# Decoder trunk on one core: a block's first weight chunk multiplied k tile by k tile, and the squares of the norm issued behind the split of x

## The chip, the cores and the metric

The kernel runs on one core of a Trainium2 chip, in one launch. The metric is the device time of one execution in microseconds (us). Input x has 256 tokens of width 1024 and stays on the chip from the first block to the last; what streams in from memory is 350 MB of weights in float32. The engines are TensorE (PE, matmuls; PEld is its weight load), VectorE (DVE), ScalarE (ACT), GpSimd (POOL) and SyncE (SP, which issues the DMAs).

## What is computed

Four layers, each of three residual steps. Mixer i mod 3 is a gated DeltaNet (layers 0 and 3, "gdn" below), a stick-breaking attention (layer 1, "sb") and a sparse attention with an indexer (layer 2, "dsa").

```python
def rmsnorm(x, g):
    y = xf * lax.rsqrt(jnp.mean(xf * xf, axis=-1, keepdims=True) + NORM_EPS)
    return (y * g).astype(x.dtype)

def swiglu(h, w_gu, w_down):
    gate, up = jnp.split(h @ w_gu, 2, axis=-1)
    return (jax.nn.silu(gate) * up) @ w_down

for i in range(DEPTH):                                   # 4
    x = x + 0.5 * swiglu(rmsnorm(x, ffn1_norm[i]), ffn1_w_gu[i], ffn1_w_down[i])
    x = x + mixer[i % 3](rmsnorm(x, mix_norm[i]))
    x = x + 0.5 * swiglu(rmsnorm(x, ffn2_norm[i]), ffn2_w_gu[i], ffn2_w_down[i])
return rmsnorm(x, final_norm)
```

D_MODEL is 1024 (8 k tiles of 128, `KT`) and D_FF is 2816.

## The kernel before

There are twelve blocks in a row, three for each layer: ffn1, mixer, ffn2. They are named here ffn1_0, gdn, ffn2_0, ffn1_1, sb, ffn2_1, ffn1_2, dsa, ffn2_2, ffn1_3, gdn (the second) and ffn2_3.

**Arithmetic.** A float32 product is made of three one-pass matmuls: both operands are split into a high part and a low part, and high x high, low x high and high x low are added in PSUM. A weight chunk is 128 x 2048 numbers; its DMA fills a raw tile `r`, and each quarter is split by ACT (L175, `h<-r`) and DVE (L176, `l<-r,h`). x is kept as eight tiles of 128 x 256. At the start of a block each of them is scaled by the gain and split by `norm_tile`: ACT writes the high part (L227) and DVE the low part (L228). One tile of products (`tile_wide`, 128 output rows by 256 tokens) is then 8 k tiles x 3 matmuls = 24 matmuls into a PSUM bank "G", of which there are four. ACT and DVE evict it (L340, L341).

**From block to block.** The last chunk of a block runs in `rows` with `last` set: after each x tile's last matmul, DVE adds the result to x (L313), and the order of the k tiles, `korder`, is the order in which the next block takes them. So the eight L313 of one block, the eight L227 and L228 of the next, and the first 24 matmuls of the next run one behind the other, a tile at a time.

**The norm.** The scale of each token (`rstd`) isn't needed for the first matmuls; it is applied to their results later. `rstd` squares x on ACT (four L249, each over two x tiles), adds the four pairs on POOL (L250 to L253, three of 128 x 512 and one of 128 x 256), sums over partitions by matmuls with a matrix of ones (rows `bankA<-ones,sq`), takes mean and inverse root on DVE (L259, then L213 to L217; in dsa a power on POOL, L262), spreads the result over the partitions by two transposes (L56, `bankA<-ident,rs_y`), and copies it to `rb` on ACT (L268). In an ffn block the evicted tiles wait for `rb`: L353 to L355 and the split of the result (L204, L205 into `ah`, `al`) stand behind it, and the first down-projection matmuls (`bankA<-ah,h`) behind those.

**What sets the order.** `rstd` is a generator that sits in a list of side work. `pump`, called after every second k tile, advances it when its due time has come on a clock `now` that counts matmul columns; `lat_sum` (5.2) is the delay between the squares and the sum, and `lat` (4.6, in an ffn block 6.6) that between the sum and the spread. The framework's scheduler then gives each engine one fixed program order; an engine takes its instructions in that order, and one that waits holds all behind it. Without a rule of its own a square (L249) is placed as soon as its two x tiles are up to date.

The first block (ffn1_0) loads x from memory and has its own start (`first_chunk`); gdn starts with eight groups of three small matmuls (16 output rows, `bah`, `bal`), sb with a product in which x is the moving operand and has 512 columns, and dsa with `project(1)` and `project(0)`, two calls of `tiles2` (two M tiles one after the other in one bank).

Of the kernel before, what the change touches and what calls it, by code (L numbers as in the profile page):

```python
# [16 lines left out]
AF = mybir.ActivationFunctionType  # L17
# [3 lines left out]
P = 128  # L21
T = 256
D = 1024
KT = D // P
# [41 lines left out]
class Trunk:  # L66
# [157 lines left out]
    def norm_tile(self, xg, n, j):  # L224
        g = self.gains[:, n, j:j + 1]
        xh, xl = xg[j]
        self.nc.scalar.activation(xh, self.x[:, j], AF.Copy, scale=g)  # L227
        self.nc.vector.scalar_tensor_tensor(xl, self.x[:, j], g, xh.bitcast(F32), op0=ALU.mult, op1=ALU.subtract)  # L228

    def norm_in(self, n):  # L230
# [13 lines left out]
    def rstd(self, st, lat=4.6, power=False):  # L244

        nc = self.nc
        sq = self.b8("sq")
        for j in range(4):
            nc.scalar.activation(sq[:, 2 * j:2 * j + 2], self.x[:, 2 * j:2 * j + 2], AF.Square)  # L249
        nc.gpsimd.tensor_add(sq[:, 0:2], sq[:, 0:2], sq[:, 2:4])  # L250
        nc.gpsimd.tensor_add(sq[:, 0:2], sq[:, 0:2], sq[:, 4:6])
        nc.gpsimd.tensor_add(sq[:, 0:2], sq[:, 0:2], sq[:, 6:8])
        nc.gpsimd.tensor_add(sq[:, 0], sq[:, 0], sq[:, 1])  # L253
        yield self.lat_sum
        b = self.bank()
        for t in range(2):
            b.mm(b.t[:, t * P:(t + 1) * P], sq[:, 0, t * P:(t + 1) * P], self.ones)
        a = self.small("ms", [P, 2])
        nc.vector.tensor_scalar(a, b.v4()[:, :2, 0], 1.0 / D, EPS, op0=ALU.mult, op1=ALU.add)  # L259
        if power:  # L260
            y = self.small("rs_y2", [P, 2])
            nc.gpsimd.tensor_tensor(y, a, self.half, op=ALU.pow)  # L262
        else:
            y = self.rsqrt(a, 2)
        yield lat
        s = self.spread([y[:, t:t + 1] for t in range(2)])
        rb = self.small("rb", [P, T])
        nc.scalar.activation(rb, s.t[:, :T], AF.Copy)  # L268
        st["rstd"], st["rb"] = y, rb
# [1 line left out]

    pool_lo = ()
    lag, width, burst = 1.0, 6, 5
    lat_sum, lat_power = 5.2, 2.4
    dsa_width = 4
    g_key, g_val, g_qry, g_del, g_new, g_inv, g_out, g_mul = 9.0, 6.0, 6.0, 8.0, 2.8, 1.0, 7.5, 1.0
    s_qk, s_sp, s_att = 2.5, 5.5, 1.3
# [2 lines left out]
                 (2, 1), (3, 2), (2, 2), (2, 3), (3, 3))  # L280
    korder = (0, 2, 4, 6, 1, 3, 5, 7)

    def tiles2(self, pieces, xg, order=None):

        b = self.bank("G")
        for m in range(2):
            for q, j in enumerate(order or self.korder):
                b.mm3(b.t[:, m * T:(m + 1) * T], self.sub(pieces, m * D + j * P, P), xg[j], q == KT - 1)
                if q % 2:
                    self.pump()  # L290
        return b

    def tile_wide(self, pieces, m, order=None):

        b = self.bank("G")
        for q, j in enumerate(order or self.korder):
            wh, wl = self.sub(pieces, m * D + j * P, P)
            xh, xl = self.x2[:, j, :T], self.x2[:, j, T:]
            b.mm(b.t[:, :T], wh, xh, False)
            b.mm(b.t[:, T:], wl, xh, False)  # L300
            b.mm(b.t[:, T:], wh, xl, q == KT - 1)
            if q % 2:
                self.pump()
        return b
# [15 lines left out]
    def ffn(self, w, n, first=False, done=None):  # L320
        nc = self.nc
        if first:
            c0, xg = self.first_chunk(w[0, 0], n)
        else:
            c0, xg = None, self.norm_in(n)
# [4 lines left out]
        def gu(s):  # L330
            for f in range(2):
                order = range(KT) if first and s + f == 0 else None
                c = c0 if c0 and s + f == 0 else self.chunk(w[s, f], parts=4 if first and s == 0 else 1)
                if first and s == 0 and f:
                    for t, src in self.consts:
                        nc.sync.dma_start(t, src)
                e = self.w5("e")
                for m in range(2):
                    b = self.tile_wide(c, m, order=order)
                    nc.scalar.activation(e[:, m * T:(m + 1) * T], b.t[:, :T], AF.Copy)  # L340
                    nc.vector.tensor_add(e[:, m * T:(m + 1) * T], e[:, m * T:(m + 1) * T], b.t[:, T:])  # L341
                late.append(e)
                if first and s + f == 0:
                    self.add(self.rstd(st, 6.6))
                if s > 0:
                    self.wait(lambda: "rb" in st)
                if "rb" in st:
                    while late:
                        acts.append(act(late.pop(0)))
# [419 lines left out]
    def dsa(self, n):  # L769
        nc, a = self.nc, self.a  # L770
# [8 lines left out]
        xg = self.norm_in(n)  # L779
# [8 lines left out]
        sq = self.b8("sq")  # L788
# [171 lines left out]
            self.split(oh[:, h], ol[:, h], bo.t[:, :T])  # L960
            heads[h] = (oh[:, h], ol[:, h])

        def project(c):
            return self.tiles2(self.chunk(a["dsa_in"][c]), xg)

        def project_q(hf):
            pieces = self.chunk(a["dsa_uq"][hf], 1536, 384)
# [7 lines left out]
                self.add(queries(2 * hf + e, b))  # L975


        b1, b0 = project(1), project(0)
        self.wait(lambda: "rb" in st)
        latents(1, b1)  # L980
        self.add(factor("fk", 2, (3,), 64, ones64, fk), 1.5)
# [6 lines left out]
        pieces = self.chunk(a["dsa_qidx"], 1536, 384)  # L988
        for pr in range(4):
            b = self.bank("G")  # L990
# [8 lines left out]
        pieces = self.chunk(a["dsa_uk"], 1536, 384)  # L999
        self.wait(lambda: {"fkv", "kidx"} <= fl)  # L1000
        for hp in range(4):
            b = self.bank("G")
# [12 lines left out]
        pieces = self.chunk(a["dsa_uv"])  # L1015
        self.width = self.dsa_width
        for t in range(2):
            ts = slice(t * P, (t + 1) * P)
            for hf in range(2):
                b = self.bank("G")  # L1020
# [197 lines left out]
```

## Time and profile before

| | us |
|---|---|
| runs | 2082.24, 2075.12, 2054.35 |
| median of the runs | 2075.12 |
| the profiled execution | 2066.59 |
| its span in the profile | 2064.6 |
| PE busy in it | 2009.8 (97%) |
| DVE, ACT, POOL busy | 1603.2 (78%), 1305.8 (63%), 163.8 (8%) |

The rows below are of the profiled execution. In a timeline row the first number is the start in us from the span's start, the second the duration; "x2" groups neighbours; matmuls overlap, so a row's duration (0.28 us) is longer than the distance to the next (0.11 to 0.12 us), and the distance of two starts is what a matmul costs. In brackets stands how long the engine was idle before the row and what released it. "a <- b: 4.9, 9, 0.7" in the view of the waits means that a waited for b for 4.9 us in all, 9 times, at most 0.7 us. The chain of waits follows the work that ended last backwards through whatever released it.

### The profile page before, as it was taken

The page shows a single profiled execution, that of the slowest core. Times are in us where ns is not written, and L with a number is a line of the kernel's source. Part 1 is how long each engine was busy: PE and PEld are TensorE (multiplying, and loading weights), DVE is VectorE, ACT ScalarE, POOL GpSimd, SP SyncE. Part 2 cuts the span into 40 slices and gives each one's busy share as a digit, 9 for nine tenths or more (in the row PEclk, how much of TensorE's full clock was granted, in tenths as well). Part 3 has the DMA queues.
Part 4 walks back from the last instruction along what each step waited for, and adds up shares of the span by engine and source line. Part 5 has one row for each costly group of instructions (what it writes and reads, how often), then busy time and mean ns, then how long its engine had stood idle before and what let it go on. Part 6 is the DMA issues. An engine that isn't in the chain of part 4 may idle for free.

```text
span 2064.6 us, 43653 instructions
## 1 busy us (share of the span) xinstructions
PE 2009.8 (97%) x17578; PEld 1978.6 (96%) x17578; DVE 1603.2 (78%) x3413; ACT 1305.8 (63%) x2804; POOL 163.8 (8%) x150
## 2 busy tenths in 40 slices
PE   8999899999999999999999998999999998999998
PEld 8999889999999989999999997999999998999998
DVE  8778898877877776866787779877787789988665
ACT  6656776666666666655666665666666667766554
POOL 1001411100100010100010023100010014201000
PEclk9999999999999999999999999999999999999999
DMA  7554323555555543555555542455555543235552
GB/s 273 191 199 170 107 104 124 184 195 193 180 209 186 202 168 139 196 184 184 184 190 199 187 161 88 165 187 201 189 195 190 198 170 103 103 123 184 184 184 82
DMA packets 52619, 353.93 MB, mean 171 GB/s; under 512 B 6976, under 2 KB 7872, under 8 KB 10688
## 3 DMA queue, kind: packets, MB, share of 16 engines
q1 hardware_dynamic: 52128, 350.49, 47.9%
q8 instruction: 137, 2.24, 0.4%
q10 hardware_dynamic: 288, 0.66, 0.1%
q14 instruction: 66, 0.54, 0.1%
HBM read 350.07 MB, written 1.05 MB: 170 GB/s over the span
## 4 chain that ended last, share of the span: by engine, by line
PE 83%; DVE 11%; ACT 3%; issue 2%; POOL 1%; DMA 0%; SPq 0%; ACTq 0%; DVEq 0%; POOLq 0%
PE bankG L43 56%; PE bankA L43 26%; DVE l L176 4%; ACT x L227 1%; DVE kT L477 1%; PE bankA L56 1%; ACT h L175 1%; DVE x L228 1%; DVE qT L477 0%; DVE x L313 0%; DVE rs_y L217 0%; DVE vT L477 0%; DVE pc L466 0%; DVE rs_t L215 0%; ACT sq L249 0%
## 5 line engine op out<-in xcount | busy, mean ns | idle before, releaser
L43 PE MATMUL bankG<-x,h 128*128 128x256 f32 x7008 | 1257.3, 280 | 9.1 <-ACT x L227 6.1
L176 DVE TENSOR_TENSOR l<-r,h 128x512 fp32r<-128x512 f32 x1328 | 936.2, 713 | 398.9 <-ACT h L175 396.8
L175 ACT ACTIVATE h<-r 128x512 fp32r<-128x512 f32 x1328 | 822.1, 626 | 575.7 <-PE bankG L43 329.1
L43 PEld LDWEIGHTS bankG<-x,h 128*128 128x128 f32 x7008 | 1077.6, 189 | 11.5 <-ACT x L227 6.4
L43 PE MATMUL bankG<-x,l 128*128 128x256 f32 x3504 | 978.4, 279 | 0.1
L43 PEld LDWEIGHTS bankG<-x,l 128*128 128x128 f32 x3504 | 659.9, 188 | 0.4 <-DVE l L176 0.3
L43 PE MATMUL bankA<-ah,h 128*128 128x256 f32 x1408 | 390.9, 278 | 0.0
L43 PE MATMUL bankA<-al,h 128*128 128x256 f32 x1408 | 390.9, 278 | 0.0
L43 PE MATMUL bankA<-ah,l 128*128 128x256 f32 x1408 | 390.8, 278 | 0.0
L43 PEld LDWEIGHTS bankA<-al,h 128*128 128x128 f32 x1408 | 266.0, 189 | 0.1
L43 PEld LDWEIGHTS bankA<-ah,h 128*128 128x128 f32 x1408 | 264.4, 188 | 0.1
L43 PEld LDWEIGHTS bankA<-ah,l 128*128 128x128 f32 x1408 | 264.4, 188 | 0.0
L341 DVE TENSOR_TENSOR e<-e,bankG 128x256 f32<-128x256 f32 x352 | 145.5, 414 | 0.9 <-ACT e L340 0.9
L340 ACT ACTIVATE e<-bankG 128x256 f32<-128x256 f32 x352 | 133.3, 379 | 7.9 <-PE bankG L43 6.3
L250 POOL TENSOR_TENSOR sq<-sq 128x512 f32<-128x512 f32 x12 | 15.5, 1290 | 1445.0 <-ACT sq L249 1445.0
L353 DVE TENSOR_TENSOR e<-e,rb 128x512 f32<-128x512 f32 x176 | 119.8, 685 | 0.0
L204 ACT ACTIVATE ah<-e 128x256 fp32r<-128x256 f32 x176 | 73.2, 417 | 22.1 <-DVE e L355 22.0
L354 ACT ACTIVATE e<-e 128x256 f32<-128x256 f32 x176 | 70.9, 404 | 14.3 <-DVE e L353 14.3
L355 DVE TENSOR_TENSOR e<-e 128x256 f32<-128x256 f32 x176 | 73.6, 419 | 0.5 <-ACT e L354 0.5
L205 DVE TENSOR_TENSOR al<-e,ah 128x256 fp32r<-128x256 f32 x176 | 73.6, 419 | 0.5 <-ACT ah L204 0.5
L43 PE MATMUL bankG<-oh,h 128*128 128x256 f32 x256 | 73.1, 286 | 0.1
L43 PE MATMUL bankG<-oh,l 128*128 128x256 f32 x256 | 71.3, 279 | 0.0
(292 smaller groups left out, 1683.0 us busy)
## 6 DMA issues: line engine op xcount, KB each, us to landing
r<-in_ffn SPq DMA_DIRECT2D x262, 1024.0 KB, 4.8
r<-in_gdn_in SPq DMA_DIRECT2D x32, 1024.0 KB, 4.8
r<-in_gdn_out SPq DMA_DIRECT2D x8, 1024.0 KB, 4.8
r<-in_sb_qk SPq DMA_DIRECT2D x8, 1024.0 KB, 4.8
r<-in_sb_v SPq DMA_DIRECT2D x4, 1024.0 KB, 5.0
r<-in_sb_out SPq DMA_DIRECT2D x4, 1024.0 KB, 4.8
r<-in_dsa_out SPq DMA_DIRECT2D x4, 1024.0 KB, 5.3
r<-in_dsa_in SPq DMA_DIRECT2D x3, 1024.0 KB, 4.8
```

What stands on the lines that cost most here:

```text
L43: self.nc.tensor.matmul(out, lhsT, rhs, start=self.fresh, stop=stop, skip_group_check=True)
L56: self.nc.tensor.transpose(out, x, self.k.ident)
L175: self.nc.scalar.activation(h[:, :pw], src, AF.Copy)
L176: (self.nc.gpsimd if pool else self.nc.vector).tensor_sub(l[:, :pw], src, h[:, :pw].bitcast(F32))
L204: self.nc.scalar.activation(dh, src, AF.Copy)
L205: self.nc.vector.tensor_sub(dl, src, dh.bitcast(F32))
L227: self.nc.scalar.activation(xh, self.x[:, j], AF.Copy, scale=g)
L340: nc.scalar.activation(e[:, m * T:(m + 1) * T], b.t[:, :T], AF.Copy)
L341: nc.vector.tensor_add(e[:, m * T:(m + 1) * T], e[:, m * T:(m + 1) * T], b.t[:, T:])
L353: nc.vector.tensor_mul(e2, e2, st["rb"][:, None, :].to_broadcast([P, 2, T]))
L354: nc.scalar.activation(e[:, :T], e[:, :T], AF.Silu)
L355: nc.vector.tensor_mul(e[:, T:], e[:, T:], e[:, :T])
```

## The change

Three things are edited. In the ffn blocks except ffn1_0, the first two output tiles are computed by `first_pair`: for each k tile the six matmuls of both M tiles, into two G banks, where before one M tile's 24 matmuls came first and then the other's. dsa's first product gets the same treatment inside one bank (`tiles2` with `first`). The four squares of `rstd` are issued under `issue_after(self.last_act)`, behind the L227 of the last x tile. And `lat_sum` goes from 5.2 to 6.5. Nothing is added or left out of the arithmetic; the number of instructions on each engine stays.

```diff
@@ norm_tile
-        self.nc.scalar.activation(xh, self.x[:, j], AF.Copy, scale=g)
+        self.last_act = self.nc.scalar.activation(xh, self.x[:, j], AF.Copy, scale=g).ins
@@ rstd
-        for j in range(4):
-            nc.scalar.activation(sq[:, 2 * j:2 * j + 2], self.x[:, 2 * j:2 * j + 2], AF.Square)
+        with self.tc.issue_after(self.last_act):
+            for j in range(4):
+                nc.scalar.activation(sq[:, 2 * j:2 * j + 2], self.x[:, 2 * j:2 * j + 2], AF.Square)
@@
-    lat_sum, lat_power = 5.2, 2.4
+    lat_sum, lat_power = 6.5, 2.4
@@ tiles2
+        if first:
+            for q, j in enumerate(self.korder):
+                w = [self.sub(pieces, m * D + j * P, P) for m in range(2)]
+                for i, o in ((0, 0), (1, 0), (0, 1)):
+                    for m in range(2):
+                        b.mm(b.t[:, m * T:(m + 1) * T], w[m][i], xg[j][o], q == KT - 1 and o == 1)
+                self.pump()
+            return b
@@
+    def first_pair(self, pieces):
+
+        bs = [self.bank("G") for _ in range(2)]
+        for q, j in enumerate(self.korder):
+            xh, xl = self.x2[:, j, :T], self.x2[:, j, T:]
+            w = [self.sub(pieces, m * D + j * P, P) for m in range(2)]
+            for m, b in enumerate(bs):
+                b.mm(b.t[:, :T], w[m][0], xh, False)
+                b.mm(b.t[:, T:], w[m][1], xh, False)
+            for m, b in enumerate(bs):
+                b.mm(b.t[:, T:], w[m][0], xl, q == KT - 1)
+            self.pump()
+        return bs
@@ ffn
+                pair = self.first_pair(c) if s + f == 0 and not first else None
                 for m in range(2):
-                    b = self.tile_wide(c, m, order=order)
+                    b = pair[m] if pair else self.tile_wide(c, m, order=order)
@@ dsa
-        b1, b0 = project(1), project(0)
+        b1 = project(1, True)
+        b0 = project(0)
```

**PE, start of ffn2_0.** The first row is the last matmul of the mixer's output projection; `x_5538` is the split x of ffn2_0. Before:

```order
L43 MATMUL bankG<-ol,h 128x256
L43 MATMUL bankG<-x_5538,h 128x256
L43 MATMUL bankG<-x_5538,l 128x256
L43 MATMUL bankG<-x_5538,h 128x256 x2
L43 MATMUL bankG<-x_5538,l 128x256
L43 MATMUL bankG<-x_5538,h 128x256 x2
```

Of the change, the same place:

```order
L43 MATMUL bankG<-ol,h 128x256
L43 MATMUL bankG<-x_5538,h 128x256
L43 MATMUL bankG<-x_5538,l 128x256
L43 MATMUL bankG<-x_5538,h 128x256
L43 MATMUL bankG<-x_5538,l 128x256
L43 MATMUL bankG<-x_5538,h 128x256 x3
L43 MATMUL bankG<-x_5538,l 128x256
L43 MATMUL bankG<-x_5538,h 128x256
L43 MATMUL bankG<-x_5538,l 128x256
L43 MATMUL bankG<-x_5538,h 128x256 x3
```

Each x tile now feeds six matmuls in a row in place of three. Further down, the matmuls with the ones (`bankA<-ones,sq`) stand behind 72 matmuls of the block in place of 60, and the spread behind 140 in place of 128; the first down-projection matmul stays behind 196.

**ACT, start of ffn2_0.** `x_5538` is L227's output, `sq` the squares, `h` a weight piece, `e` an eviction. Before:

```order
L227 ACTIVATE x_5538<-x,gains 128x256 x4
L175 ACTIVATE h<-r 128x512
L227 ACTIVATE x_5538<-x,gains 128x256
L249 ACTIVATE sq<-x 128x512
L227 ACTIVATE x_5538<-x,gains 128x256 x2
L249 ACTIVATE sq<-x 128x512
L227 ACTIVATE x_5538<-x,gains 128x256
L249 ACTIVATE sq<-x 128x512 x2
L175 ACTIVATE h<-r 128x512
L340 ACTIVATE e<-bankG 128x256
```

Of the change (the squares are now L250, the eviction L364):

```order
L227 ACTIVATE x_5538<-x,gains 128x256 x4
L175 ACTIVATE h<-r 128x512
L227 ACTIVATE x_5538<-x,gains 128x256
L175 ACTIVATE h<-r 128x512
L227 ACTIVATE x_5538<-x,gains 128x256 x2
L175 ACTIVATE h<-r 128x512
L227 ACTIVATE x_5538<-x,gains 128x256
L250 ACTIVATE sq<-x 128x512 x4
L175 ACTIVATE h<-r 128x512 x3
L364 ACTIVATE e<-bankG 128x256 x2
```

The places of the first two squares, ahead of the last three x tiles, are taken by two weight pieces; all four squares follow the eighth x tile.

**ACT, start of the first gdn.** `x_2669` is its split x. Before:

```order
L227 ACTIVATE x_2669<-x,gains 128x256
L249 ACTIVATE sq<-x 128x512
L227 ACTIVATE x_2669<-x,gains 128x256 x2
L249 ACTIVATE sq<-x 128x512
L227 ACTIVATE x_2669<-x,gains 128x256
L249 ACTIVATE sq<-x 128x512 x2
L175 ACTIVATE h<-r 128x512
L162 ACT_TABLE_LOAD
```

Of the change:

```order
L227 ACTIVATE x_2669<-x,gains 128x256
L175 ACTIVATE h<-r 128x512
L227 ACTIVATE x_2669<-x,gains 128x256 x2
L162 ACT_TABLE_LOAD
L227 ACTIVATE x_2669<-x,gains 128x256
L250 ACTIVATE sq<-x 128x512 x4
L175 ACTIVATE h<-r 128x512 x7
```

Here a load of ACT's function table has moved ahead of the eighth x tile. In sb and dsa it stands right behind the eighth x tile and ahead of all four squares; before, two squares stood ahead of it. In gdn the sum keeps its place behind 72 matmuls and the spread behind 96; in sb the sum moves from 36 to 42 and the spread from 54 to 58, in dsa from 60 to 72 and from 86 to 98.

## Rows read from the trace of the kernel before

**Rows 1.** The page's line of the clock granted to PE, in 40 slices of the span (9 is 90% of full speed or more).

```profile
PEclk9999999999999999999999999999999999999999
```

**Rows 2.** The view of the waits, whole span: what PE waited for at the spread, and its weight loads at block starts (us in total, times, longest us).

```profile
PE bankA L56 <- DVE rs_y L217: 11.5, 10, 2.2
...
PEld bankG L43 <- DVE x L228: 4.9, 9, 0.7
```

**Rows 3.** The timeline of PE in ffn2_0: its first matmul, the matmul at the eighth x tile and the next one, the sum of squares, and the first down-projection matmul.

```profile
373.99 0.28 PE L43 MATMUL bankG<-x,h 128*128 128x256 f32 x1
...
376.58 0.28 PE L43 MATMUL bankG<-x,l 128*128 128x256 f32 x1
377.06 0.51 PE L43 MATMUL bankG<-x,h 128*128 128x256 f32 x2 [0.20 <-DVE x L228]
...
381.39 0.60 PE L43 MATMUL bankA<-ones,sq 128*128 128x128 f32 x4
...
397.05 0.28 PE L43 MATMUL bankA<-ah,h 128*128 128x256 f32 x1
```

**Rows 4.** The timeline of ACT at the start of ffn2_0.

```profile
373.42 0.61 ACT L249 ACTIVATE sq<-x 128x512 f32<-128x512 f32 x1
373.94 0.89 ACT L227 ACTIVATE x<-x,gains 128x256 fp32r<-128x256 f32 x2
374.74 0.61 ACT L249 ACTIVATE sq<-x 128x512 f32<-128x512 f32 x1
375.26 0.49 ACT L227 ACTIVATE x<-x,gains 128x256 fp32r<-128x256 f32 x1
375.66 1.14 ACT L249 ACTIVATE sq<-x 128x512 f32<-128x512 f32 x2
```

**Rows 5.** The timelines of DVE and of POOL there, one after the other; the last DVE row is the split of a result that the down projection takes first.

```profile
375.79 1.22 DVE L228 SCALAR_TENSOR_TENSOR x<-x,gains,x 128x256 fp32r<-128x256 f32 x1 [0.29 <-ACT x L227]
376.93 1.78 DVE L176 TENSOR_TENSOR l<-r,h 128x512 fp32r<-128x512 f32 x1
...
393.73 0.42 DVE L205 TENSOR_TENSOR al<-e,ah 128x256 fp32r<-128x256 f32 x1
...
375.43 1.29 POOL L250 TENSOR_TENSOR sq<-sq 128x512 f32<-128x512 f32 x1 [32.92 <-ACT sq L249]
376.80 1.36 POOL L251 TENSOR_TENSOR sq<-sq 128x512 f32<-128x512 f32 x1
378.24 1.63 POOL L252 TENSOR_TENSOR sq<-sq 128x512 f32<-128x512 f32 x1
379.94 1.07 POOL L253 TENSOR_TENSOR sq<-sq 128x256 f32<-128x256 f32 x1
```

**Rows 6.** The chain of waits (start us, us, what): long pieces of it with nothing but PE, ahead of ffn2_0, in ffn2_0 and in ffn2_1.

```profile
362.84 9.56 PE bankG L43 x81
...
402.65 10.88 PE bankG L43 x96
...
874.32 11.31 PE bankG L43 x96
```

**Rows 7.** The view by stretches, ffn2_1 and then ffn1_2 from after their start to before their end (stretch, its length, and then for each engine busy us and instructions, PEclk, share of DMA, GB/s).

```profile
845.00:1031.00 186.00, 185.62 (x1577) 185.42 (x1576) 137.04 (x266) 112.20 (x231) 5.36 (x4) 1.00 0.53 187
1033.00:1212.00 179.00, 178.79 (x1576) 178.59 (x1575) 136.68 (x265) 111.72 (x230) 5.34 (x4) 1.00 0.55 193
```

**Rows 8.** Timelines at the start of the first gdn: ACT's second square and its table load, POOL's last add, and PE at the eighth x tile, at the sum and at the spread.

```profile
191.22 0.61 ACT L249 ACTIVATE sq<-x 128x512 f32<-128x512 f32 x1
...
193.82 1.28 ACT L162 ACT_TABLE_LOAD   x1
...
196.41 1.07 POOL L253 TENSOR_TENSOR sq<-sq 128x256 f32<-128x256 f32 x1
...
193.55 0.29 PE L43 MATMUL bankA<-x,bah 128*16 128x256 f32 x1 [0.17 <-DVE x L228]
...
199.21 0.61 PE L43 MATMUL bankA<-ones,sq 128*128 128x128 f32 x4
...
203.01 0.43 PE L56 MATMUL bankA<-ident,rs_y 128*128 128x128 f32 x2 [0.60 <-DVE rs_y L217]
```

**Rows 9.** Timelines at the start of sb (the first four) and of dsa (the others): POOL's last add, the sum and the spread on PE, and ACT's squares behind its table load.

```profile
742.70 1.07 POOL L253 TENSOR_TENSOR sq<-sq 128x256 f32<-128x256 f32 x1
...
743.93 0.61 PE L43 MATMUL bankA<-ones,sq 128*128 128x128 f32 x4
...
738.84 1.15 ACT L249 ACTIVATE sq<-x 128x512 f32<-128x512 f32 x2
...
750.38 0.43 PE L56 MATMUL bankA<-ident,rs_y 128*128 128x128 f32 x2 [2.16 <-DVE rs_y L217]
...
1216.42 1.15 ACT L249 ACTIVATE sq<-x 128x512 f32<-128x512 f32 x2
...
1221.26 0.71 PE L43 MATMUL bankA<-ones,sq 128*128 128x128 f32 x4 [0.37 <-POOL sq L253]
...
1225.05 0.43 PE L56 MATMUL bankA<-ident,rs_y 128*128 128x128 f32 x2 [0.34 <-POOL rs_y L262]
```

**Rows 10.** Timelines at the start of the first block, ffn1_0: an ACT square ahead of the first x tiles, and DVE's last four L228.

```profile
4.98 0.63 ACT L249 ACTIVATE sq<-x 128x512 f32<-128x512 f32 x1
...
9.20 2.39 DVE L228 SCALAR_TENSOR_TENSOR x<-x,gains,x 128x256 fp32r<-128x256 f32 x4 [0.23 <-ACT x L227]
```

More of the change, by code (lines that the diff above doesn't have):

```diff
@@ L281, with tiles2 @@
     korder = (0, 2, 4, 6, 1, 3, 5, 7)
-    def tiles2(self, pieces, xg, order=None):
+    def tiles2(self, pieces, xg, order=None, first=False):
         b = self.bank("G")
+        if first:
[6 more added lines that the diff above has]
+            return b
         for m in range(2):
@@ L961, in attend, with project @@
             heads[h] = (oh[:, h], ol[:, h])
-        def project(c):
-            return self.tiles2(self.chunk(a["dsa_in"][c]), xg)
+        def project(c, first=False):
+            return self.tiles2(self.chunk(a["dsa_in"][c]), xg, first=first)
         def project_q(hf):
```

## The prediction

> **What bounds the kernel now.** I read the page first. PE is busy for 97% of the span and the clock granted to it is 9 in all 40 slices [rows 1], its upper level; time can only come from PE's few idle stretches, or from the spacing of its matmuls. Next the view of the waits, for what PE idles on: the split of x at block starts (nine waits of PE's weight loads for L228, 4.9 us, 0.54 us each) and the spread's wait for the inverse root (11.5 us) [rows 2]. Then the timelines of one block start after another, and the chain of waits over whole blocks.
>
> In ffn2_0 the matmul at the eighth x tile starts at 376.58 and the next at 377.06, 0.48 us where 0.12 is usual [rows 3]. ACT shows why the tile is late: its last L227 starts at 375.26, behind a square that started at 374.74 [rows 4]. DVE adds to it: its last L228 took 1.22 us while POOL's first add (375.43 to 376.72) ran [rows 5].
>
> One more thing stands in the chain. In ffn2_0, 96 matmuls take 10.88 us (113.3 ns each), in ffn2_1 11.31 us (117.8 ns) [rows 6], at the same granted clock and with DVE and ACT equally busy [rows 7]. The same 1576 matmuls or so need 179 us in ffn1_2 and 186 in ffn2_1 [rows 7]. So PE has two cadences, 7 us per ffn block apart. Ahead of ffn2_0 it ran the slow one (81 matmuls in 9.56 us, 118.0 ns) and behind the wait at the eighth tile the fast one [rows 6]; a block seems to keep what it has after such a wait.
>
> **The change, part by part.**
>
> *k tile by k tile (first_pair).* PE takes an x tile in 3 x 0.117 = 0.35 us and wants the eighth 21 matmuls after 373.99, at 376.5; it was there at 375.79 + 1.22 = 377.0 [rows 3, 5]. With six matmuls per tile it is wanted 42 matmuls after 373.99, at 378.8. I take the stall as gone in all seven ffn blocks: 7 x 0.54 = **-3.8 us** [rows 2]. What covers a late tile is then 1.8 us of matmuls; a tile later by more than that would bring the stall back. No weight piece is late: both M tiles use the chunk that was split before the block starts.
>
> *Squares behind the split, in ffn blocks.* In ACT's queue weight pieces (about 0.62 us) take the places of the two early squares (0.61), so the eighth L227 stays at 375.26. The first square follows at 375.66, the second at 376.18 and ends at 376.79 (spacing 0.52 by [rows 4]). POOL starts 0.08 us behind the second square, as before (375.35 to 375.43), and its chain takes from 375.43 to 381.01, 5.58 us [rows 5]. So the last add ends near 376.87 + 5.58 = 382.45, 1.44 us later than before. PE reaches the sum behind 72 matmuls in place of 60, at 373.99 + 72 x 0.1133 = 382.15. It waits some 0.30 us and 0.07 for the signal: 0.37 us, and all matmuls of the block stand behind it. In the slow cadence PE arrives at 382.47 and waits for next to nothing. Seven times 0.37 is **+2.6 us**. Bounds: 0, if POOL's chain is on time; and +0.62 more per block (+4.3) if one more weight piece gets ahead of a square.
>
> Behind the sum, mean, root, spread and `rb` move later by about 1.4 us, as the spread does (128 to 140 matmuls), so that I see no wait there; the first split result is ready at 394.15 and first used at 397.05 [rows 3, 5], 2.9 us, of which 1.5 stay. Cost nothing; if that cover were gone, it would be PE waiting for `al`, with 1600 matmuls behind.
>
> The lock between DVE and POOL moves with the squares. L228 is free of it; the weight pieces that follow (1.78 us for one L176 in place of about 0.7 [rows 5]) get it, as they do now. The Trainium skill, SBUF — State Buffer, section Who interferes with whom, says that a VectorE instruction with two SBUF inputs and a GpSimd one that reads SBUF exclude each other for a whole instruction; the 1.22 and 1.78 us agree. By that rule the last L228 costs 0.48 us, and the sum is as here.
>
> *ffn1_0.* The square at 4.98 delays the first x split by 0.52 us and the first matmul with it, and the last four L228 took 2.39 us [rows 10] where four free ones take about 1.7. Both go: **-1.0 us**, bounds 0 and -1.3 (0.52 + 0.7).
>
> *gdn, twice.* The matmuls keep their order; the table load now stands ahead of the eighth x tile. ACT is through with the seventh by 191.3, where the second square stood; the load takes 1.28 [rows 8]; the eighth L227 starts at 192.6, and its L228, no longer blocked by POOL, ends at 193.6: the stall that ended at 193.55 stays within 0.1. The second square starts at 193.5 in place of 191.22, 2.3 us later, and POOL ends at 199.8 in place of 197.48. PE wants it at 199.3, 0.1 later than now: 0.5 and 0.07, and 0.1. The spread already waits 0.60 for the root, so nothing hides this: 0.7 each, **+1.4 us** (bounds 0, if POOL is quicker, and +3, if on top one more weight split, 0.7, gets ahead of the mean).
>
> *sb.* The squares start behind the table load, at 738.84; the second ends at 739.98, POOL at 740.06 + 5.58 = 745.64 in place of 743.77. PE is there at 743.93 + 6 x 0.23 = 745.3: +0.4. The spread waits 2.16 for the root [rows 9]; four matmuls moved ahead of it take 0.9 out of that wait, and the root comes up to 1.8 later. **+0.4 us**, bounds -0.9 and +0.9.
>
> *dsa.* The first square moves to 1216.42, the second ends at 1217.56; POOL is done at 1223.1, 1.9 us later than before. The sum moves from 1221.26 to 1223.2 [rows 9], but 12 matmuls (1.36 us) are done ahead of it: **+0.55 us**, and the root's wait of 0.34 stays. Bounds -1 and +1.
>
> Sum: -3.8 + 2.6 - 1.0 + 1.4 + 0.4 + 0.55 = **+0.15 us**. Against its own time, 2066.6 us (span 2064.6 and 2.0 around it), that is 2066.7. The median of the runs lies 8.5 us higher, and the runs lie 28 us apart, which is four ffn blocks of 7 us: I read them as 0 to 4 blocks in the slow cadence (two, ffn2_1 and ffn2_3, in the profiled execution). The mean over the four executions is 2069.6; with +0.15 I predict **2070 us**.
>
> **The rivals.**
>
> *1. The squares are in time.* POOL's three adds of one shape take 1.29, 1.36 and 1.63 us [rows 5]; if all took 1.29, the chain would be 0.41 shorter and end at 382.04, ahead of 382.15. Then only the signal's 0.07 is left at each sum, 0.5 for the seven, and each mixer's term is 0.4 smaller: -3.8 + 0.5 - 1.0 + 0.6 + 0 + 0.15 = -3.5, **2066 us**. Against it: DVE's splits lie beside the long adds, and just as many of them do after the change.
>
> *2. The sum becomes the bound (slower).* Where POOL ends more than 0.54 us behind PE's arrival, a block loses more than the stall gave. One weight piece more ahead of the squares and one more lock on DVE or POOL (0.62 + 0.7) put the wait at 1.7: 7 x (1.7 - 0.54) = +8.1, with +4 in the mixers and -1 in ffn1_0: **2081 us**. For it: only 0.3 us separate the two now. Against it: ACT's order is fixed and has no weight piece there.
>
> *3. The cadence.* The waits at block starts are where the cadence changed. If they go and nothing takes their place, each block keeps what the block before left: ffn2_0 and ffn1_1 slow, ffn2_1 and ffn1_2 fast, one block more in the slow cadence, or two, +7 to +14 us: **2080 us**; if all seven ran slow, 5 x 7 = +35, **2105**; if all were fast, -14, **2056**. For it: the change of cadence at 377.06. Against it: the sum's interruption of 0.37 us may change the cadence as well. The Trainium skill, TensorE: Matmul & The Clock Gate, section Back-to-back issue gap, gives one spacing, N / 2.4 + 2.5 ns, 109.2 ns for 256 columns, for isolated matmuls at the full clock. With one spacing there is no such term and the time is 2066.7; the trace has 113.3 and 117.8, so it differs.
>
> **How the numbers follow.** Forecast (gains and new waits cancel) 0.45; rival 1 0.2; rival 2 0.1; rival 3 0.25, of which 0.15 slower, 0.1 faster. A measurement of this kernel can tell about 2% (41 us) from no change, since its own runs lie 28 us apart. More than 2% faster would be under 2034, which no case reaches: 0.02. More than 2% slower is over 2117, all blocks slow and rival 2 on top: 0.02. Within 2%: 0.96. The likeliest one's own range is 2064 to 2076, by the bounds of its terms. The range goes from all blocks fast with rival 1 (2052) to two more slow blocks and half of rival 2 (2089).
>
> **What the profile after would show.** The first 48 matmuls of an ffn block at even spacing with no wait for L228; a wait of 0.3 to 0.5 us at the matmuls with the ones, released by POOL's last add; the spread without one in the ffn blocks; ACT's table load ahead of the eighth x tile in gdn; waits for POOL at the sum in gdn, sb and dsa. Wrong would be the prediction if the waits at the sum were over 1 us, if the down projection waited for `al`, or if most ffn blocks ran at one cadence.

## The result and the profile after

| | before | the change |
|---|---|---|
| runs, median | 12 runs, 2058.16 us | 12 runs, 2070.86 us |
| lowest and highest | 2054.34 to 2082.24 | 2067.51 to 2078.14 |
| span of the profiled execution | 2064.6 | 2076.2 |
| ratio | | 1.0053 (95% interval 1.003 to 1.0075) |

The change makes the kernel 0.5% slower, 6 to 15 us. The predicted 2070 us agrees with the measured time by luck, because the starting point was put too high: four executions of before had a mean of 2069.6, twelve have a median of 2058.16. The forecast that gains and new waits cancel was wrong. How large the loss is depends on the set of runs taken of before: in the four sets that ran beside the experiments (23 to 29 runs each) its median was 2062.92 to 2066.35, which would leave 4.5 to 8 us. The lowest time of before is steadier, 2052.38 to 2055.25 over all five sets, 12 to 15 us under the lowest of the change.

The view of the waits of the changed kernel no longer has the row of PE's weight loads on L228 [rows 2]. In its place PE waits eleven times for POOL's last add:

```profile
PE bankA L56 <- DVE rs_y L217: 13.6, 10, 2.2
PEld bankA L43 <- POOL sq L254: 11.1, 11, 1.2
PE bankA L43 <- POOL sq L254: 8.7, 11, 1.0
```

The last two rows are the same eleven waits, seen at the weight load and at the matmul. 4.9 us of waiting became 11.1, 1.0 each. The timeline of PE in ffn1_1 of the change shows the place; it answers to [rows 3]:

```profile
558.88 0.28 PE L43 MATMUL bankG<-x,h 128*128 128x256 f32 x1
...
568.18 0.71 PE L43 MATMUL bankA<-ones,sq 128*128 128x128 f32 x4 [0.99 <-POOL sq L254]
568.65 0.36 PE L43 MATMUL bankG<-x,h 128*128 128x256 f32 x1
...
576.51 0.38 PE L56 MATMUL bankA<-ident,rs_y 128*128 128x128 f32 x2
...
582.88 0.28 PE L43 MATMUL bankA<-ah,h 128*128 128x256 f32 x1
```

PE comes to the sum at 558.88 + 72 x 0.1133 = 567.04, as predicted, and starts it at 568.18: 1.14 us lost. The down projection begins 24.0 us into the block, against 23.06 in ffn2_0 before [rows 3]. ACT, DVE and POOL of the same stretch, one after the other, answer to [rows 4, 5]:

```profile
559.70 0.62 ACT L175 ACTIVATE h<-r 128x512 fp32r<-128x512 f32 x1
560.22 0.49 ACT L227 ACTIVATE x<-x,gains 128x256 fp32r<-128x256 f32 x1
560.62 2.18 ACT L250 ACTIVATE sq<-x 128x512 f32<-128x512 f32 x4
...
560.74 0.48 DVE L228 SCALAR_TENSOR_TENSOR x<-x,gains,x 128x256 fp32r<-128x256 f32 x1 [0.22 <-ACT x L227]
561.15 7.53 DVE L176 TENSOR_TENSOR l<-r,h 128x512 fp32r<-128x512 f32 x6
...
561.83 1.76 POOL L251 TENSOR_TENSOR sq<-sq 128x512 f32<-128x512 f32 x1 [175.45 <-ACT sq L250]
563.67 1.63 POOL L252 TENSOR_TENSOR sq<-sq 128x512 f32<-128x512 f32 x1
565.38 1.62 POOL L253 TENSOR_TENSOR sq<-sq 128x512 f32<-128x512 f32 x1
567.08 1.05 POOL L254 TENSOR_TENSOR sq<-sq 128x256 f32<-128x256 f32 x1
```

The last L228 is back at 0.48 us and POOL starts 2.95 us into the block (predicted 2.88). But the chain then takes 6.30 us (561.83 to 568.13) and not 5.58: the first add is 1.76 instead of 1.29, the second 1.63 instead of 1.36, beside a row of six weight splits that take 7.53 us, 1.25 each. The last two adds take what they took before. It is so in all seven ffn blocks: 6.2 to 6.3 us in the change, 5.6 in before. The first add used to run beside the last L228; the second ran beside a split before as well, and why it then took only 1.36 is not shown. The chain of waits runs through exactly these adds:

```profile
563.67 1.64 POOL sq L252
565.38 1.62 POOL sq L253
567.08 1.06 POOL sq L254
568.18 0.71 PE bankA L43 x4
568.90 7.78 PE bankG L43 x66
...
588.48 10.88 PE bankG L43 x96
```

Behind the sum 66 matmuls take 7.78 us, 117.9 ns each, the slow cadence; from the spread on it is the fast one. In ffn1_2 the slow one stays, as the view by stretches shows for ffn2_1 and ffn1_2 (columns as in [rows 7]; PE's instruction count is in the first bracket):

```profile
851.00:1031.00 180.00, 179.01 (x1577) 178.82 (x1577) 137.38 (x266) 111.99 (x230) 6.07 (x4) 1.00 0.55 194
1033.00:1219.00 186.00, 185.01 (x1573) 184.82 (x1572) 137.28 (x264) 111.91 (x230) 6.06 (x4) 1.00 0.52 186
```

In gdn (timelines of ACT, POOL and PE, against [rows 8]) the table load stands ahead of the eighth x tile, POOL ends at 200.85, and the spread waits 1.04 in place of 0.60:

```profile
192.42 1.28 ACT L162 ACT_TABLE_LOAD   x1
193.71 0.51 ACT L227 ACTIVATE x<-x,gains 128x256 fp32r<-128x256 f32 x1
...
199.79 1.06 POOL L254 TENSOR_TENSOR sq<-sq 128x256 f32<-128x256 f32 x1
...
200.90 0.71 PE L43 MATMUL bankA<-ones,sq 128*128 128x128 f32 x4 [0.78 <-POOL sq L254]
...
205.16 0.43 PE L56 MATMUL bankA<-ident,rs_y 128*128 128x128 f32 x2 [1.04 <-DVE rs_y L217]
```

The time of each block, from its first x matmul to that of the next block (PE's timeline; s marks a block whose long run was in the slow cadence, judged by the spacing of its 256-column matmuls):

| block | before | change | k-tile order alone (e1) | adds on DVE (e9) |
|---|---|---|---|---|
| ffn1_0 | 184.34 | 185.84 | 187.50 | 190.98 s |
| gdn | 183.58 | 185.71 | 183.84 | 182.14 |
| ffn2_0 | 180.82 | 181.68 | 180.23 | 180.23 |
| ffn1_1 | 180.88 | 181.76 | 180.23 | 180.23 |
| sb | 108.98 | 109.28 | 109.01 | 106.08 |
| ffn2_1 | 187.78 s | 181.76 | 180.23 | 180.23 |
| ffn1_2 | 180.82 | 188.16 s | 180.23 | 180.23 |
| dsa | 106.79 | 106.73 | 106.77 | 105.01 |
| ffn2_2 | 180.93 | 188.16 s | 180.23 | 180.23 |
| ffn1_3 | 180.90 | 181.42 | 180.23 | 180.23 |
| gdn, second | 183.76 | 186.44 | 184.36 | 182.94 |
| ffn2_3, to the end of the span | 199.00 s | 193.62 | 191.54 | 191.54 |

Of one cadence, an ffn block costs 0.5 to 0.9 us more in the change, the two gdn blocks 2.1 and 2.7, ffn1_0 1.5 (it starts 0.4 earlier), sb 0.3, dsa nothing. Both profiles have two slow ffn blocks, so the 11.6 us between the spans aren't the cadence's.

Single blocks scatter without any change. On PE, ACT, DVE and POOL the order of the first block is the same in before and in e6 (the experiments are described below), and it took 184.34 and 186.53 us; that of the gdn blocks is the same in before, e1, e6 and e8, and the first took 182.50 to 183.84, the second 183.76 to 184.61. A difference of 1 to 2 us in one of these blocks between two profiles is therefore not yet the change's.

### The profile page after: what moved, and what is told of

Same layout as the page of the kernel before. It is cut to its first block, busy times and chain, and to the rows that moved or that the text cites. A ratio compares the mean times of both kernels' runs of the same rounds, so it can differ in the third digit from the quotient of the medians.

```text
span 2076.2 us, 43666 instructions
## 1 busy us (share of the span) xinstructions
PE 2017.2 (97%) x17578; PEld 1986.2 (96%) x17578; DVE 1606.0 (77%) x3413; ACT 1307.6 (63%) x2804; POOL 167.7 (8%) x150
## 4 chain that ended last, share of the span: by engine, by line
PE 82%; DVE 10%; ACT 3%; POOL 3%; issue 2%; DMA 0%; SPq 0%; DVEq 0%; ACTq 0%; POOLq 0%
PE bankG L43 54%; PE bankA L43 26%; DVE l L176 3%; DVE kT L501 1%; PE bankA L56 1%; ACT h L175 1%; ACT x L227 1%; ACT sq L250 1%; POOL sq L253 1%; POOL sq L252 1%; DVE x L336 1%; POOL sq L254 0%; DVE x L228 0%; DVE qT L501 0%; DVE rs_t L216 0%
## 5 line engine op out<-in xcount | busy, mean ns | idle before, releaser
L176 DVE TENSOR_TENSOR l<-r,h 128x512 fp32r<-128x512 f32 x1328 | 946.5, 721 | 406.4 <-ACT h L175 404.8
L364 ACT ACTIVATE e<-bankG 128x256 f32<-128x256 f32 x352 | 133.0, 380 | 8.6 <-PE bankG L43 6.8
```

The source lines that it names most:

```text
L176: (self.nc.gpsimd if pool else self.nc.vector).tensor_sub(l[:, :pw], src, h[:, :pw].bitcast(F32))
```

## The experiments

Theory S: the squares' chain on POOL ends too late, and PE waits for it at the sum. Rival P: the k-tile order itself costs. Rival C: all is the cadence.

**e1: the k-tile order alone.**

```diff
-        with self.tc.issue_after(self.last_act):
-            for j in range(4):
-                nc.scalar.activation(sq[:, 2 * j:2 * j + 2], self.x[:, 2 * j:2 * j + 2], AF.Square)
+        for j in range(4):
+            nc.scalar.activation(sq[:, 2 * j:2 * j + 2], self.x[:, 2 * j:2 * j + 2], AF.Square)
```

> The change with the squares back at their old places (no rule that puts them behind the split); the k-tile order and lat_sum 6.5 stay. Theory S (the time was lost because the squares' POOL chain ends 9.25 us behind a block's first matmul while PE comes to the sum of squares at 8.2): the chain ends near 7.1 again, PE does not wait at the sum, and the x stall is gone too; lowest and median time 3 to 5 us under before, ratio 0.997 to 0.999. Rival P (the k-tile order itself costs, in banks, evictions or weights): as slow as the change, ratio 1.004 to 1.007. Rival C (nothing but the cadence of PE's matmuls, fast or slow for a whole block): the lowest time equals that of before, and the view by stretches shows more slow blocks than before.

Median 2066.44, lowest 2050.57; before beside it 2066.35 and 2052.38; ratio 1.000 (0.9967 to 1.0034). The timelines of PE and of POOL in ffn1_1 show the sum without a wait, 1 us behind POOL's end:

```profile
565.74 0.60 PE L43 MATMUL bankA<-ones,sq 128*128 128x128 f32 x4
...
563.60 1.07 POOL L253 TENSOR_TENSOR sq<-sq 128x256 f32<-128x256 f32 x1
```

All seven ffn blocks take 180.23 us, 0.6 to 0.7 less than before in the same cadence. So the k-tile order gains what the stall cost, and P falls. In the median, where 3 to 5 us were expected, that gain can't be seen: the twelve times spread over 30 us.

**e2: the squares' rule alone**, on the kernel before.

```diff
-        self.nc.scalar.activation(xh, self.x[:, j], AF.Copy, scale=g)
+        self.last_act = self.nc.scalar.activation(xh, self.x[:, j], AF.Copy, scale=g).ins
...
+        with self.tc.issue_after(self.last_act):
```

> Before with the squares behind the split alone; M tiles one after the other, lat_sum 5.2. Theory S: the sum stands behind 60 matmuls (6.8 us) and POOL ends near 9.25, so PE waits about 2.4 us at the sum in each of seven ffn blocks, and the x stall of 0.5 is mostly gone since the last low part of x no longer meets a POOL add: +1.9 x 7 and +5 to +6 in gdn and the first block, 18 us over before, ratio 1.007 to 1.010. Rival P: the loss belongs to the k-tile order, so this one is within 3 us of before, ratio 0.999 to 1.002. Rival C: lowest time equal to before.

Median 2088.47, lowest 2081.65; ratio 1.0112 (1.0077 to 1.0147). The loss belongs to the rule, and is larger with the earlier sum; 1.007 to 1.010 was expected. Not all of it is the wait. PE at the sum and a stretch behind it, in ffn2_0 and then in ffn1_1:

```profile
384.69 0.71 PE L43 MATMUL bankA<-ones,sq 128*128 128x128 f32 x4 [2.32 <-POOL sq L254]
...
386.00:388.00 2.00, 2.00 (x20) 2.00 (x20) 1.76 (x9) 1.52 (x3) 0.00 (x0) 1.00 0.86 266
...
567.50 0.71 PE L43 MATMUL bankA<-ones,sq 128*128 128x128 f32 x4 [2.32 <-POOL sq L254]
...
569.00:571.00 2.00, 2.00 (x11) 2.00 (x11) 1.76 (x10) 1.14 (x3) 0.00 (x0) 0.50 0.90 299
```

After the same wait of 2.32 us the granted clock stayed at 1.00 (2.4 GHz) in one block and was 0.50 (1.2 GHz) in the other; it fell in four of the seven ffn blocks. In the fast cadence a block where it stayed takes 182.81 us, and one where it fell 184.4.

**e3: the sum later.**

```diff
-    lat_sum, lat_power = 6.5, 2.4
+    lat_sum, lat_power = 8.0, 2.4
```

> The change with lat_sum 8.0 in place of 6.5: in an ffn block the sum stands behind 84 matmuls (9.5 us) in place of 72, the spread behind 146 in place of 140. Theory S: POOL's end at 9.25 is covered, the wait of about 1.0 at the sum goes in seven ffn blocks; mean and root move by at most 0.3 us and stay ahead of the spread and the down projection: about 7 us under the change, lowest near 2060, ratio to before 1.001 to 1.003. If the chain behind the sum is as tight as the sum itself (root late for the spread, or the split results late for the down projection), the wait moves there and the time stays at 1.005. Rival C: no change of the lowest time against the change.

Median 2072.84, lowest 2065.48; ratio 1.0035 (1.0006 to 1.0065). Block by block S holds: four ffn blocks of the profile take 180.23, the others are slow (187.2), and no later wait appeared. PE at the sum of ffn1_1:

```profile
566.39 0.28 PE L43 MATMUL bankG<-x,h 128*128 128x256 f32 x1
566.50 0.60 PE L43 MATMUL bankA<-ones,sq 128*128 128x128 f32 x4
```

The times don't follow: the lowest was expected near 2060, and the median is no lower than the change's. In the profile the slow cadence comes out of dsa and stays for the two ffn blocks behind it, and comes out of the second gdn and stays again.

**e4: the sum earlier**, `lat_sum` 5.2 in the change.

```diff
-    lat_sum, lat_power = 6.5, 2.4
+    lat_sum, lat_power = 5.2, 2.4
```

> The change with lat_sum back at 5.2: in an ffn block the sum stands behind 60 matmuls (6.8 us) and the spread behind 128. Theory S: POOL still ends near 9.25, the wait at the sum grows from 1.0 to 2.4 us in seven ffn blocks: +9 to +10 us over the change, ratio to before 1.009 to 1.012. Rival P and rival C: the place of the sum matters little, within 2 us of the change.

Median 2087.05, lowest 2086.26; ratio 1.0102 (1.0075 to 1.013). Six ffn blocks take 184.4, 2.7 more than in the change, where about 1.4 was expected for the 12 matmuls fewer ahead of the sum. The other half is the clock; PE's timeline at the sum of ffn1_1, and two stretches behind it:

```profile
575.14 0.80 PE L43 MATMUL bankA<-ones,sq 128*128 128x128 f32 x4 [2.31 <-POOL sq L254]
...
576.17 0.63 PE L43 MATMUL bankG<-x,h 128*128 128x256 f32 x2
576.60 0.41 PE L43 MATMUL bankG<-x,l 128*128 128x256 f32 x1
...
576.00:579.00 3.00, 3.00 (x16) 3.00 (x16) 2.83 (x10) 1.09 (x3) 0.00 (x0) 0.50 0.74 248
...
583.00:586.00 3.00, 3.00 (x29) 3.00 (x28) 1.90 (x5) 1.91 (x4) 0.00 (x0) 1.00 0.45 186
```

After a wait of 2.31 us the granted clock is 0.50 for the next 3 us, and a matmul takes 213 ns; 15 of them cost 1.5 us. It fell so in all seven ffn blocks of e4, against four of seven in e2; what makes the difference is not shown.

**e5: the rule in the ffn blocks only.**

```diff
-        with self.tc.issue_after(self.last_act):
+        with (self.tc.issue_after(self.last_act) if behind else contextlib.nullcontext()):
...
-        self.add(self.rstd(st, 6.6))
+        self.add(self.rstd(st, 6.6, behind=True))
```

> The change with the squares' rule in the ffn blocks alone (the first one too); in gdn, sb and dsa the squares are back between the x tiles. Theory S by block: the two gdn blocks, 185.7 and 186.4 us in the change against 183.6 and 183.8 before, go back to 183.6 to 183.9; sb and dsa stay within 0.4; the ffn blocks stay at 181.7 (fast cadence): lowest time about 4 to 5 us under the change's 2067.5, ratio to before 1.002 to 1.004. If the gdn blocks' loss is not the squares' (the order behind them, or the cadence of their many short stretches), the gdn blocks stay at 185 to 186.5.

Median 2062.10, lowest 2057.65; ratio 0.9978 (0.9955 to 1.0002), lower than expected. The gdn blocks take 183.59 and 185.36 (185.71 and 186.44 in the change): the first as expected, the second only halfway, which is within the scatter of these blocks. sb fell to 107.09, which the rule doesn't explain, and only one ffn block was slow.

**e6: e1 with the first block's sum at its old place.**

```diff
-        yield self.lat_sum
+        yield lat_sum or self.lat_sum
...
-                    self.add(self.rstd(st, 6.6))
+                    self.add(self.rstd(st, 6.6, lat_sum=5.2))
```

> The k-tile order without the squares' rule, lat_sum 6.5, but 5.2 in the first block, where 6.5 had moved the sum from 108 to 120 matmuls. Theory S: the first block comes back from 187.5 to 184.0 to 184.4 us, the seven ffn blocks stay at 180.2 (fast cadence), the mixers as before: lowest time 2048 to 2050, 3 to 4 us under the lowest of before; median 3 to 7 us under before, ratio 0.996 to 0.999, as far as the cadence lets it be seen. If the first block's loss in the first experiment had another cause, it stays at 187 to 188.

Lowest 2048.11, as expected; median 2069.65; ratio 0.9995 (0.9956 to 1.0034). The ffn blocks are 180.23 again, but ffn1_0 took 186.53, not 184.0 to 184.4, though its order is again that of before: the place of the sum doesn't explain it. The median, expected 3 to 7 us under that of before (2063.51), lies 6 above it. The times fall apart, five from 2048 to 2056 and seven from 2069 to 2086.

**e7: POOL's last add left out**, its work done by two matmuls more.

```diff
-        nc.gpsimd.tensor_add(sq[:, 0], sq[:, 0], sq[:, 1])
...
-            b.mm(b.t[:, t * P:(t + 1) * P], sq[:, 0, t * P:(t + 1) * P], self.ones)
+            b.mm(b.t[:, t * P:(t + 1) * P], sq[:, 0, t * P:(t + 1) * P], self.ones, False)
+            b.mm(b.t[:, t * P:(t + 1) * P], sq[:, 1, t * P:(t + 1) * P], self.ones)
```

> The change with POOL's fourth add (128 x 256, 1.05 us) left out: the sum over partitions takes both halves by four matmuls in place of two. Theory S: POOL ends near 8.2 us, just when PE arrives behind 72 matmuls, the wait at the sum falls from 1.05 us to 0.1 or less, the two matmuls more cost 0.45: ffn blocks (fast cadence) 181.7 to about 181.1, gdn 0.5 less too: 5 to 7 us under the change, ratio to before 0.999 to 1.003. If PE's wait at the sum is not set by POOL's last add, the two matmuls more make it 4 to 5 us slower than the change.

Median 2102.10; ratio 1.0164 (1.0129 to 1.02): 30 us worse than forecast. Yet the wait went as S says; POOL and PE in ffn2_0, then stretches of ffn2_0 and ffn2_1:

```profile
391.50 1.62 POOL L253 TENSOR_TENSOR sq<-sq 128x512 f32<-128x512 f32 x1
...
393.17 1.16 PE L43 MATMUL bankA<-ones,sq 128*128 128x128 f32 x8
...
405.00:570.00 165.00, 165.00 (x1404) 165.00 (x1403) 117.21 (x225) 97.85 (x200) 0.00 (x0) 1.00 0.54 190
...
885.00:1045.00 160.00, 160.00 (x1414) 160.00 (x1413) 118.44 (x226) 98.36 (x202) 0.00 (x0) 1.00 0.55 194
```

PE waits for nothing worth a row (the gap ahead of the sum is 130 ns where 117 is usual), and the one fast ffn block, ffn2_1, takes 180.79. But seven of eight ffn blocks are slow: 165 us for 1404 matmuls, against 160 for 1414. So the cadence alone can cost some 30 us, with no wait of note.

**e8: e1 with the sum behind 60 matmuls.**

```diff
-    lat_sum, lat_power = 6.5, 2.4
+    lat_sum, lat_power = 5.2, 2.4
```

> The k-tile order without the squares' rule and with lat_sum 5.2 everywhere: the sum stands behind 60 matmuls (6.8 us) and POOL ends near 7.09. Theory S alone: a wait of 0.3 to 0.4 us at the sum, ffn blocks in the fast cadence 180.5 to 180.6, so that the lowest time is 2050 to 2051 and the median some 2 us over that of the version with the sum behind 72. Theory C beside it (a wait at the sum changes the cadence for what follows, no wait keeps it): the share of slow ffn blocks differs clearly from that of the versions with no wait at the sum, most blocks slow (median over 2080, as with three adds) or most fast (median under 2058).

Median 2058.30, lowest 2053.28; ratio 0.9978 (0.9955 to 1.0002). PE in ffn1_1:

```profile
567.34 0.71 PE L43 MATMUL bankA<-ones,sq 128*128 128x128 f32 x4 [0.18 <-POOL sq L253]
```

A wait of 0.34 us per block (starts 566.89 and 567.34, less 0.11), ffn blocks of 180.7, and still a ratio that is no higher than that of e1 (1.000), which waits for nothing. The lowest time is 2 us above the expected one, but the times bunch (2053 to 2068, where e1 had 2051 to 2080), nearly as C says: the median was to be under 2058.

**e9: the change with the adds on VectorE.**

```diff
-        nc.gpsimd.tensor_add(sq[:, 0:2], sq[:, 0:2], sq[:, 2:4])
+        nc.vector.tensor_add(sq[:, 0:2], sq[:, 0:2], sq[:, 2:4])
```

and the other three adds likewise.

> The change with the four adds of the squares on VectorE in place of POOL: four instructions of about 0.69, 0.69, 0.69 and 0.42 us, no second engine that shares a port with VectorE. If the chain's 6.3 us in the change is POOL's slower adds and the exclusion between the two engines, the sum's input is ready by about 7 us, the wait of 1.05 us at the sum goes, weight splits (L176) beside the adds take 0.69 in place of 1.8, ffn blocks fast cadence 180.2 to 180.4, lowest time 6 to 9 us under the change's. If VectorE has no room for 2.5 us more of work at a block's start, weight splits come late, PE waits for L176, and the blocks stay at 181.5 or more.

Median 2055.66, lowest 2042.92, before beside it 2063.07 and 2054.2; ratio 0.9968 (0.9938 to 0.9997). DVE and PE in ffn1_1, whose first matmul is at 558.75:

```profile
561.02 1.28 DVE L176 TENSOR_TENSOR l<-r,h 128x512 fp32r<-128x512 f32 x2
562.23 0.68 DVE L251 TENSOR_TENSOR sq<-sq 128x512 f32<-128x512 f32 x1
...
564.63 0.68 DVE L253 TENSOR_TENSOR sq<-sq 128x512 f32<-128x512 f32 x1
...
565.57 0.41 DVE L254 TENSOR_TENSOR sq<-sq 128x256 f32<-128x256 f32 x1
...
566.92 0.60 PE L43 MATMUL bankA<-ones,sq 128*128 128x128 f32 x4
```

The adds take 0.68 us each, two weight splits 1.28 together, and the sum's input is ready 7.2 us into the block, with the squares where the change put them. No wait; ffn blocks 180.23; sb and dsa 2 to 3 us shorter than before, gdn 0.8 to 1.4. So the late chain was POOL's, and its cost was on both engines. The lowest time lies 24.6 us under the change's, where 6 to 9 were expected: in the profiles the mixers alone gained 12 us on the change (gdn 3.6 and 3.5, sb 3.2, dsa 1.7), which was not forecast.

**e10: the adds on VectorE in e6.**

```diff
-        nc.gpsimd.tensor_add(sq[:, 0:2], sq[:, 0:2], sq[:, 2:4])
+        nc.vector.tensor_add(sq[:, 0:2], sq[:, 0:2], sq[:, 2:4])
```

> The k-tile order, the squares at their old places, lat_sum 6.5 but 5.2 in the first block, and the four adds on VectorE. Theory S: ffn blocks 180.2 as in the version with POOL, no wait anywhere at block starts; gdn, sb and dsa up to 1 us shorter each, since the mean comes earlier; lowest time 2045 to 2049. Theory C: as no wait changes the cadence, the times spread over 2046 to 2085 as they did there, with a median of 2060 to 2070.

Median 2062.74, lowest 2042.69; ratio 0.9968 (0.9934 to 1.0001). The lowest is 11.5 us under that of before, and 2 us below the expected bound; the spread is as C says.

**e11 and e12: a wait put back, by an earlier sum**, `lat_sum` 4.6 and 4.0 in e10.

```diff
-    lat_sum, lat_power = 6.5, 2.4
+    lat_sum, lat_power = 4.6, 2.4
```

> As the version before it (k-tile order, squares at their old places, adds on VectorE, 5.2 kept only where it was in the first block) with lat_sum 4.6: the sum stands behind 54 matmuls, 6.12 us, and the adds end at 6.30. Theory S alone: a wait of 0.2 to 0.3 us in seven ffn blocks, lowest time 2 us over that version's 2042.7, median 2 us over its 2062.7. Theory C: a wait at the sum is a new draw of the cadence in every ffn block where no wait keeps what the block before left. If the draw is mostly fast, as with the sum behind 60 and POOL, the times bunch at 2045 to 2060 with a median of 2050 to 2055; if it is mostly slow, as with three adds, the median is over 2080.

> The same with lat_sum 4.0: the sum stands behind 51 matmuls, 5.78 us, and the wait for the adds is 0.5 to 0.6 us in seven ffn blocks. Theory S alone: lowest time 4 us over the 2042.7 of the version without a wait. Theory C: again a draw in every block; the share of slow blocks is near that of the run with 54 if the kind of interruption decides, and differs from it if the draw hangs on the exact length of the wait.

e11: median 2058.25, lowest 2052.13, ratio 0.9988 (0.9963 to 1.0013). e12: 2061.99, 2052.65, 0.9989 (0.9965 to 1.0014). The ffn blocks in the fast cadence take 180.5 to 180.6 and 180.9 to 181.0; one of eight is slow in either profile. The median of e11 is 4.5 us under e10's, where S alone had it 2 over, and still above the 2050 to 2055 that C had for a mostly fast draw. The times bunch more than in e10, but the lowest is nearly 10 us higher and not 2 or 4: with a draw in each block, hardly a run has all of them fast. That reason is argued from the one slow block in either profile; the lowest executions left no trace.

**The cadence over all traces.** I took the spacing of the 256-column matmuls on both sides of the sum in ffn blocks. Where PE waits for nothing at the block's start and at the sum (e1, e3, e6, e9, e10; 35 blocks), the cadence behind the sum is the one ahead of it, 35 times. Behind a wait of 0.2 to 1.2 us met in the fast cadence it is fast in 19 of 29 (the change 0 of 5, e5 4 of 6, e8 5 of 6, e11 4 of 5, e12 6 of 7); behind a lag of about 15 ns (e7) in 1 of 4. Of three such waits met in the slow cadence (the change, e5) one led to the fast one; e2 and e4, where the clock fell too, are left out. The runs agree in part: mean less lowest time is 14 to 17 us in e1, e6, e9 and e10, and 4.5 to 9 in the change, e5, e8, e11 and e12; e3, without waits too, has 9.3, and before, which waits for x at every block start, 7.8 to 13.8 in its five sets. The rule isn't strict: in e11 two slow blocks turned fast at a sum with no gap over 120 ns ahead of it, and at the spread seven slow blocks turned fast with no wait (four in the change, two in e5, one in e8). That a wait sets the cadence is thus argued, not shown.

## Why the prediction was wrong

- **The x stall goes, -3.8 us: right.** 0.6 to 0.7 us per ffn block in e1.
- **"Squares behind the split, in ffn blocks", +2.6 us: this step failed, by its size.** The mechanism, PE's arrival and POOL's start were right. The chain was taken over from before at 5.58 us; it measured 6.30, since the first two adds now run beside weight splits (1.76 and 1.63 us in place of 1.29 and 1.36), where the first used to run beside the last x tile's low part. I had moved the lock with the squares for DVE and not for POOL. The wait is 1.14 us in the fast cadence and 0.76 in the slow one, in place of 0.37, about 7 us for seven blocks. The matmuls from the sum to the spread ran slow on top in six of them, 66 x 4.5 ns = 0.3 us each. e9, where only the engine of the adds is changed, removes both. The sign that I had named for being wrong, a wait of over 1 us at the sum, came true.
- **No wait behind the sum: right.** Spread and down projection show none in the ffn blocks.
- **gdn, +1.4 us for both: too small.** Measured 2.1 and 2.7. The sum starts 0.6 and 0.8 us later in the block, near the forecast, but the spread waits longer too and starts 1.07 later; that much is shown. The chain itself is not longer here (5.5 us). The rest lies within the scatter: the blocks in which PE and DVE have before's order (before, e1, e5, e6, e8) take 183.3 and 184.5 on average, those with the change's order (the change, e2, e3, e4) 184.8 and 185.8, which makes 1.5 and 1.3 and not 2.1 and 2.7.
- **ffn1_0, -1.0 us: not confirmed.** It starts 0.4 us earlier and takes 1.5 longer. The spread comes at 26.0 us of the block in place of 22.3, the down projection at 29.9 in place of 26.3, behind 20 and 17 matmuls more. But the block takes 184.3 to 187.5 in the traces with fast cadence, with different waits at its first loads, and 186.53 in e6 with the very order of before. So neither a gain nor a loss of the change can be read from it, and the cause of the 1.5 us stays open.
- **sb +0.4, dsa +0.55:** measured +0.3 and -0.06.
- **Rival 2 was the nearest**: its threshold (POOL ends more than 0.54 us behind PE) was passed, with 1.09 us (567.04 to 568.13), by the longer adds and not by a weight piece. It was given 0.1 because ACT's order was fixed, while the margin was 0.3 us on a chain of 5.6.
- **Rival 3** holds in part: without a wait at the block's start and at the sum the cadence stayed in 35 of 35 blocks, and behind a wait it often changed; but it also changed without one. In the profiles it didn't decide the sign, both having two slow blocks; but it hides gains: e1 and e6 save 4 us in seven ffn blocks and don't show it in the median.

Added up by blocks the change loses 7 x about 0.75 + 4.8 (gdn) + 1.1 (ffn1_0) + 0.25 (sb, dsa) = 11.4 us, against 11.6 between the spans. Shown to be the squares' rule are the seven ffn blocks and about 2 us of the gdn blocks; the rest is open.

## What to carry to other kernels

When work is moved in time, price it again beside its new neighbours: a chain on GpSimd that met short VectorE instructions before may meet long ones after, and both get slower. A chain that ends 0.3 us from where TensorE wants it is not hidden; give it another engine (with the adds on VectorE, 0.68 us each in place of a chain of 6.3 us on GpSimd, the change was 0.3% faster than before, 95% interval 0.03 to 0.6%, and not 0.5% slower). A later place took the wait away too, but the times of e3 didn't fall with it. And compare blocks of one cadence, not only medians, when two executions of one program differ by more than the change is worth; first look how far a block differs between profiles in which nothing of it was changed.

## What the runs showed of the hardware that was not expected

- A stream of weight load and 256-column matmul pairs runs at 113.3 or at 117.8 ns per pair at the same granted clock, for 1500 matmuls on end, with DVE and ACT equally busy. In e7 it changed in three of four blocks at a sum that came 15 ns late; whether the lag or the two added matmuls did it, and what picks the one or the other, isn't shown.
- After a wait of 2.3 us the granted clock was 0.50 for some 3 us in all seven ffn blocks of e4 and in four of seven of e2, and stayed at 1.00 in the other three; after one of 1.0 us (the change) it stayed at 1.00.
- A 128x512 add on POOL took 1.29 us beside one 128x256 L228, which itself took 1.22 in place of 0.48, and 1.6 to 1.76 beside 128x512 weight splits, which themselves took 1.25 in place of 0.64; the same add on DVE took 0.68.
